# One list schedule for mixers, projections and MLP, with tiles placed late

## The chip, the cores and the metric

The kernel runs on one core of a Trainium2 chip. The metric is the device time of one execution in microseconds. The engines of the core work beside each other, each on its own instruction stream: TensorE (PE, matmuls, with its weight loads shown apart as PEld), VectorE (DVE), ScalarE (ACT), GpSimd (POOL), and SyncE (SP), which here only issues DMAs. Matrix products are accumulated in PSUM, whose banks have to be read out by DVE or ACT before they are used again.

## The reference

One inference step of a layer with four mixers in parallel, over 128 context and 512 latent tokens of width 1024 (640 token rows in all):

```python
h = rmsnorm(x, norm1_g) * (1 + scale1) + shift1
proj = h @ w_in
(a_q, a_i, a_ff, a_fb, a_g, b_q, b_k, b_v, b_g, b_af, b_ab,
 c_x, c_g, d_b, d_c, d_v) = jnp.split(proj, points, axis=-1)
o_a, sf_a = hgrn2_mixer(a_q, a_i, a_ff, a_fb, a_g, ...)      # gated linear recurrence
o_b, sf_b = gla_mixer(b_q, b_k, b_v, b_g, b_af, b_ab, ...)   # gated linear attention
o_c, sf_c = rglru_mixer(c_x, c_g, ...)                       # gated recurrent block
o_d = short_conv_mixer(d_b, d_c, d_v, sconv_w, rows)         # gated short convolution
mix = jnp.concatenate([o_a, o_b, o_c, o_d], axis=-1) @ w_out
x = x + gate1 * mix
h2 = rmsnorm(x, norm2_g) * (1 + scale2) + shift2
ff = jnp.square(jax.nn.relu(h2 @ mlp_w1)) @ mlp_w2
x = x + gate2 * ff
```

Scale, shift and gate come from a conditioning vector for each kind of token. The recurrences of A and B run in both directions in chunks of 32 tokens; their final states are outputs, too. A last rmsnorm follows. w_in is 1024 wide on the input side, w_out 1024x1024, the MLP 1024 to 4096 and back.

## The kernel before, in words

Each large product is made in fp32r with split operands: a matrix is rounded to a high part (`hi`), the rest is the low part (`lo`), and hi·hi, hi·lo and lo·hi are added in PSUM. So a weight tile costs a DMA, a rounding copy (ACT or DVE) and a subtraction (DVE) before PE can use it. The scores and states of the recurrences, the head norms, sums and transposes are plain fp32 matmuls.

The program has four stretches.

1. Start, to about 50 us: x is loaded, normed, transposed and split (`hhi`, `hlo`); first projections. An order written by hand (`START`, under `manual_schedule`, L416) sets it.
2. Mixers and input projections, about 50 to 324 us. The string `PLAN` (L33) lists the units: a projection of 128 columns (`proj_cm`, L229, into the PSUM tiles `pja`, `pjbqk`, `pjcx`, ..., `pjdv`, `pjdb`; values `vi` and `vbv` at L599 to L601), or one step of a generator that runs a mixer (A0, A1, B, RG). Scores are `sA`, `sB` (L699, L726), sums for the conditioning `ap` (L273, L279), gates of the recurrent block `rg` (L869), head norms `hna`, `hnb` (L808). Instructions are written in the order of the list; the framework's own scheduler then orders them on each engine, and places tiles at the point where the program asks for them.
3. Out-projection, 324 to about 367 us. `out_mm` (L1055, its matmuls at L1070) handles one of 5 token tiles and one of 8 row blocks k of w_out; blocks are taken in the order `kord` = 4, 5, 0, 1, 2, 3, 6, 7. Half of the blocks have their split weights in tiles `xh`, `xl` (loaded as `wq` by `wo_x`, L1014 to L1016), half in `vh`, `vl` (loaded as `w2raw` by `wo_v`, L1020). Blocks 4, 5, 2, 3 are in `xh`, blocks 0, 1, 6, 7 in `vh`. `wq` lies in a pool that is opened behind the close of the mixers' and the projections' pools (`ml_`, `hw_`), `w2raw` and `vh` in one that only needs the earlier mixer pool.
4. MLP, to 820 us, with sums and differences of blocks of h2 and of w1 that save products (`product`, matmuls at L1241) and a second product (`mm2`, L1321). Its weights are `wq` to `xh`, `xl` (L1224, L1225) and `w2raw` to `vh`, `vl` (L1311, L1312); operands derived from h are `yh`, `yl`, `ohi`, `t` (L1137, L1138).

Stretches 3 and 4 are ordered by the class `Plan` (L53 to L143): each unit is added with an engine, a duration and what it reads and writes; PE's units stay chained in the order of the program; the rest are placed by a list schedule, earliest start first, and among the startable the one with the earliest latest-start time. Units were bundles (one `out_mm` of 6 matmuls is one entry of 1.36 us).

Of the kernel before, what the change touches and what calls it, by code (L numbers as in the profile page):

```python
# [51 lines left out]

class Plan:  # L53
# [3 lines left out]
    def __init__(self):  # L57
        self.ops = []
        self.writer, self.readers = {}, {}

    def add(self, eng, dur, fn, r=(), w=(), late=0.0):
        i = len(self.ops)
        deps = set()
        for k in r:
            if k in self.writer:
                deps.add(self.writer[k])
        for k in w:
            if k in self.writer:
                deps.add(self.writer[k])
            deps.update(self.readers.get(k, ()))  # L70
        for k in r:
# [5 lines left out]
        self.ops.append((eng, dur, fn, deps, late))  # L77

    def emit(self):
        n = len(self.ops)  # L80
        hop = 0.13
        pe_t, t = {}, 0.0
        for i, (eng, dur, *_) in enumerate(self.ops):
            if eng == "PE":
                pe_t[i] = t
                t += dur
        end = t
        latest = [pe_t.get(i, end + 10.0) for i in range(n)]
        prev = {}
        lastpe = None  # L90
        for i in range(n):
            if i in pe_t:
                prev[i] = lastpe
                lastpe = i
        for i in range(n - 1, -1, -1):
            eng, dur, fn, deps, late = self.ops[i]
            for d in deps:
                e2, d2, _, _, l2 = self.ops[d]
                need = latest[i] - d2 - l2 - (hop if e2 != eng else 0.0)
                latest[d] = min(latest[d], need)  # L100
        left = [len(o[3]) for o in self.ops]
        after = [[] for _ in range(n)]
        for i, o in enumerate(self.ops):
            for d in o[3]:
                after[d].append(i)
            if prev.get(i) is not None and prev[i] not in o[3]:
                left[i] += 1
                after[prev[i]].append(i)
        ready = {}
        at = [0.0] * n  # L110
        free = {}
        for i in range(n):
            if not left[i]:
                ready.setdefault(self.ops[i][0], []).append(i)
        order = []
        while len(order) < n:
            best = None
            for eng, xs in ready.items():
                if not xs:
                    continue  # L120
                f = free.get(eng, 0.0)
                s = max(f, min(at[i] for i in xs))
                i = min((x for x in xs if at[x] <= s + 1e-9), key=lambda x: (latest[x], x))
                if best is None or s < best[0]:
                    best = (s, eng, i)
            s, eng, i = best
            ready[eng].remove(i)
            _, dur, fn, deps, late = self.ops[i]
            free[eng] = s + max(dur - 0.08, 0.05)
            order.append((s, i))  # L130
            for j in after[i]:
                e2 = self.ops[j][0]
                d = s + dur + late + (hop if e2 != eng else 0.0) if i in self.ops[j][3] else free[eng]
                if e2 == eng and eng != "SP" and i in self.ops[j][3]:
                    d = free[eng]
                at[j] = max(at[j], d)
                left[j] -= 1
                if not left[j]:
                    ready.setdefault(e2, []).append(j)
        self.order = order  # L140
        for _, i in order:
            self.ops[i][2]()
# [3 lines left out]
def hybrid_step_kernel(ctx: ExitStack, tc: tile.TileContext, A: dict, O: dict):  # L146
# [42 lines left out]
    def lnexp(after):  # L189
        with tc.issue_after(after.ins):  # L190
            ld = act.preload_act_table_set("natural_log_exp_and_others")
        with tc.issue_after(ld.ins):
            yield
# [253 lines left out]
    me = me_.enter_context(tc.tile_pool(name="mixe", bufs=1, reuse_waits="tile"))  # L447
    mp = ml_.enter_context(tc.tile_pool(name="mixl", bufs=1, side="right", reuse_waits="tile"))
# [7 lines left out]
    def sub(t, g, off, ap):  # L456
        v = t[:, g, off:off + 1]
# [489 lines left out]
    for u in PLAN:  # L947
# [10 lines left out]
        if u == "q1":  # L958
            psS_stack.close()
            psB = stB.enter_context(tc.tile_pool(name="psB", bufs=2, space=PS, reuse_waits="tile"))  # L960
    grow1 = gate_rows("gt1", nc.sync)
    for j in jobs.values():
        assert next(j, None) is None
    me_.close()
    lp = ctx.enter_context(tc.tile_pool(name="mlp", bufs=1, reuse_waits="tile"))
# [16 lines left out]
    ls = ctx.enter_context(tc.tile_pool(name="mlps", bufs=1, reuse_waits="tile"))  # L982
    stB.close()
    psA_.close()
    psN = ctx.enter_context(tc.tile_pool(name="psN", bufs=1, space=PS, reuse_waits="tile"))
# [4 lines left out]
    def tiles(p, n, shape, nm, dt=F32):  # L990
        return [p.tile([128] + shape, dt, name=f"{nm}{i}", tag=f"{nm}{i}") for i in range(n)]
# [14 lines left out]
    XA = {}  # L1006
# [614 lines left out]
```

## Time and profile before

| | |
|---|---|
| median of 3 runs | 828.07 us (824.24 to 829.06) |
| the profiled execution's own time | 829.46 us |
| its span, first to last instruction | 827.7 us |
| mean granted TensorE clock over the span | 0.989 of full speed |
| busy: PE, DVE, ACT, POOL | 783.6, 581.2, 425.9, 23.5 us |
| DMA | 97.78 MB, 118 GB/s on average |

Busy time says how long an engine had an instruction in work. PE's busy time overstates what it needed, since matmuls overlap and their ends are modelled; where PE is back to back, the distance between starts is the better measure. A wait is put down to the instruction that ended last before it was over. The chain of waits follows the program back from its last instruction, at each step to what released it.

### The profile page before, as it was taken

To read this page: it belongs to the slowest core of one execution; us is meant where nothing else is said; L and a number is where in the kernel's file an instruction comes from. 1 tells how busy PE (TensorE), PEld (TensorE's weight loads), DVE (VectorE), ACT (ScalarE), POOL (GpSimd) and SP (SyncE) were. 2 spreads that over 40 slices of the span, in tenths; PEclk is the share of its full clock that TensorE was granted. 3 is DMA by queue.
4 is the path that set the end of the run, shared out by engine and by line. 5 is a ranking of instruction groups with operands and counts; after the bars stand their busy time and mean duration, and the time that the engine had idled before them with its cause. 6 is when DMAs were issued, how large, how long until landed. Compare 5 with 4: busy or idle time off the path is not lost.

```text
span 827.7 us, 13723 instructions
## 1 busy us (share of the span) xinstructions
PE 783.6 (95%) x5536; PEld 688.0 (83%) x5536; DVE 581.2 (70%) x1061; ACT 425.9 (51%) x708; POOL 23.5 (3%) x48
## 2 busy tenths in 40 slices
PE   4999999999989987999799999999999999999996
PEld 3798987777777987888797989989899898988984
DVE  4789989767875466177888898947567475563787
ACT  7543559688396323156566734717247173471533
POOL 0040000101010000000000000000000000000001
PEclk9999999999999999999999999999999999999998
DMA  9723333342411522434444534444132041330313
GB/s 369 286 96 116 104 127 109 112 152 57 151 52 55 123 81 81 174 128 139 166 153 128 178 103 153 115 113 130 51 114 91 16 138 51 101 103 1 126 53 127
DMA packets 33695, 97.78 MB, mean 118 GB/s; under 512 B 8672, under 2 KB 9696, under 8 KB 29024
## 3 DMA queue, kind: packets, MB, share of 16 engines
q1 hardware_dynamic: 32544, 95.72, 34.7%
q10 hardware_dynamic: 576, 1.00, 0.4%
q8 instruction: 43, 0.70, 0.3%
q0 software_dynamic: 512, 0.20, 0.1%
q14 instruction: 20, 0.16, 0.1%
HBM read 91.44 MB, written 5.46 MB: 117 GB/s over the span
## 4 chain that ended last, share of the span: by engine, by line
PE 65%; DVE 14%; ACT 12%; DMA 6%; issue 2%; SPq 0%; DVEq 0%; ACTq 0%
PE ps L1321 26%; PE ps L1241 20%; PE ps L1070 5%; ACT QbB L199 2%; PE pjcx L229 2%; PE pjdb L229 2%; PE pja L403 2%; DMA w2raw<-in_wout_dram 1%; DMA wq<-in_w_dram 1%; DVE QbB L197 1%; PE pjdv L229 1%; DMA rawdb<-in_win_dram 1%; PE ap L273 1%; DVE StA L771 1%; ACT QbA L199 1%
## 5 line engine op out<-in xcount | busy, mean ns | idle before, releaser
L1321 PE MATMUL ps<-vh,olo 128*128 128x512 f32 x640 | 173.7, 390 | 0.5 <-DVE olo L1267 0.5
L1321 PEld LDWEIGHTS ps<-vh,olo 128*128 128x128 f32 x640 | 119.5, 188 | 26.0 <-DVE olo L1267 1.7
L1321 PE MATMUL ps<-vl,olo 128*128 128x512 f32 x320 | 99.2, 389 | 0.0
L1311 ACT ACTIVATE vh<-w2raw 128x1024 fp32r<-128x1024 f32 x32 | 33.7, 1057 | 121.6 <-PE ps L1321 114.1
L1241 PE MATMUL ps<-yh,xh 128*128 128x320 f32 x256 | 79.8, 312 | 1.0 <-DVE rb L1283 1.0
L1241 PE MATMUL ps<-yh,xl 128*128 128x320 f32 x256 | 79.7, 311 | 0.0
L1241 PE MATMUL ps<-yl,xh 128*128 128x320 f32 x256 | 79.6, 311 | 0.0
L1516 DVE TENSOR_TENSOR h<-ps,h 128x512 f32<-128x512 f32 x60 | 38.5, 685 | 56.7 <-PE ps L1321 56.3
L1224 ACT ACTIVATE xh<-wq 128x512 fp32r<-128x512 f32 x96 | 58.4, 625 | 24.0 <-PE ps L1241 17.6
L1225 DVE TENSOR_TENSOR xl<-wq,xh 128x512 fp32r<-128x512 f32 x96 | 64.1, 686 | 9.3 <-ACT xh L1224 8.9
L1321 PEld LDWEIGHTS ps<-vl,olo 128*128 128x128 f32 x320 | 60.1, 188 | 12.6
L1241 PE MATMUL ps<-ohi,xh 128*128 128x320 f32 x256 | 58.6, 316 | 4.6 <-ACT rb L1280 4.6
L1241 PEld LDWEIGHTS ps<-yh,xh 128*128 128x128 f32 x256 | 48.6, 190 | 1.6 <-DVE rb L1283 1.3
L1241 PEld LDWEIGHTS ps<-yl,xh 128*128 128x128 f32 x256 | 48.6, 190 | 0.3
L1241 PEld LDWEIGHTS ps<-yh,xl 128*128 128x128 f32 x256 | 48.5, 189 | 0.0
L1241 PEld LDWEIGHTS ps<-ohi,xh 128*128 128x128 f32 x256 | 43.8, 192 | 5.5 <-ACT rb L1280 5.1
L1280 ACT ACTIVATE rb<-ps 128x320 f32<-128x320 f32 x64 | 27.3, 428 | 40.5 <-PE ps L1241 38.9
L1312 DVE TENSOR_TENSOR vl<-w2raw,vh 128x1024 fp32r<-128x1024 f32 x32 | 38.7, 1221 | 11.2 <-ACT vh L1311 10.5
L1241 PE MATMUL ps<-ohi,xl 128*128 128x320 f32 x128 | 40.2, 314 | 0.0
L1267 DVE TENSOR_TENSOR olo<-rb,olo 128x640 fp32r<-128x640 f32 x32 | 26.3, 821 | 16.1 <-ACT olo L1266 16.1
L1241 PE MATMUL ps<-t,xh 128*128 128x320 f32 x128 | 28.6, 310 | 1.2 <-DVE rb L1283 1.2
L1283 DVE TENSOR_TENSOR rb<-ps,rb 128x320 f32<-128x320 f32 x48 | 23.3, 487 | 7.0 <-PE ps L1241 6.1
(438 smaller groups left out, 1731.7 us busy)
## 6 DMA issues: line engine op xcount, KB each, us to landing
ar<-in_ada_w_dram SPq DMA_DIRECT2D x20, 1024.0 KB, 4.8
wq<-in_w_dram SPq DMA_DIRECT2D x72, 256.0 KB, 3.5
w2raw<-in_w_dram SPq DMA_DIRECT2D x32, 512.0 KB, 4.3
big<-in_ada_g_dram SPq DMA_DIRECT2D x8, 512.0 KB, 3.6
x<-in_x_dram SPq DMA_DIRECT2D x5, 512.0 KB, 5.6
big<-in_x_dram SPq DMA_DIRECT2D x5, 512.0 KB, 4.4
x1d<-big SPq DMA_DIRECT2D x5, 512.0 KB, 2.7
xa<-x1d SPq DMA_DIRECT2D x5, 512.0 KB, 4.5
```

The costliest lines, as they stand in the source:

```text
L199: act.activation(out, src, AF.Copy)
L229: pe.matmul(ps[:, n, :320], wt[:, k, c0:c0 + 128], h[:, k, s], start=(k == 0 and wt is hi and h is hhi), stop=stop)
L1070: pe.matmul(ps[n], lh, w[ix[n]] if nm == "x" else w[ix[0]][:, HALVES[n]], start=(ki == 0 and i == 0), stop=(ki == 7 and i == 2))
L1224: plan.add(ACT, aa_(512), lambda: act.activation(hi, src, AF.Copy), sk, [("xh", s)])
L1225: plan.add(DVE, tt(512), lambda: dve.tensor_tensor(lo, src, hi.bitcast(F32), OP.subtract), sk + [("xh", s)], [("xl", s)])
L1241: pe.matmul(PT[b][n][:, :HT], w[:, k, :], h[:, k, :], start=(start and k == 0 and i == 0), stop=(k == 3 and i == 2), skip_group_check=True)
L1267: plan.add(DVE, tt(640), lambda: dve.tensor_tensor(AL[i], r, AH[i].bitcast(F32), OP.subtract), rk + [("ah", i)], [("al", i)])
L1280: plan.add(ACT, 0.44, lambda: act.activation(dst, src, AF.Copy), [r], [w])
L1311: plan.add(ACT, aa_(1024), lambda hi=hi, raw=raw: act.activation(hi, raw, AF.Copy), rk, [("vh", i)])
L1312: plan.add(DVE, tt(1024), lambda hi=hi, lo=lo, raw=raw: dve.tensor_tensor(lo, raw, hi.bitcast(F32), OP.subtract), rk + [("vh", i)], [("vl" ...
L1321: pe.matmul(PT[b][c.start // 512], lh[i][:, ts_], rh[i][:, c], start=(i == 0 and pi == 0), stop=(i == 3 and pi == 2))
L1516: DVE, tt(512), lambda: dve.tensor_tensor(a, PT[b][n], a, OP.add), [pk[n], ("h", n)], [("h", n)]))
```

## The change

The class `Plan` now records everything behind the start: mixers, input projections, the splitting of their outputs, the loads and splits of w_out, out-projection and MLP. Calls on the engines go through proxies (`Engine`, `Queues`) that record one instruction each with a modelled cost. Tiles of the recorded part are placeholders (`LateTile`) and get a real place when the schedule reaches their first user; the order in which tiles of one tag take slots stays that of the program. Pools are opened by events in the schedule. PE's instructions of the mixers may be put in any order that the data allow; from the out-projection on they stay chained. The loads of ACT's tables are put in by the schedule, at a price of 1.28 us, and a switch counts as 6 us of lateness. In the out-projection, blocks 4, 5, 0, 1 now have `vh`, `vl`, and blocks 2, 3, 6, 7 `xh`, `xl`. In the very last tile, both halves' last multiplication come after both halves' sums.

```diff
+class LateTile:
+    def place(self):
+        if self.got is None:
+            shape, dtype, name, tag, bufs = self.args
+            self.got = self.pool.real.tile(shape, dtype, name=name, tag=tag, bufs=bufs)
+        return self.got
...
+    def cost(self, eng, op, out, ins, a, k):
...
+        if eng == "PE":
+            if op == "transpose":
+                return 4 * self.size(ins[0]) / 2400, 0.0
+            cols = self.size(a[2])
+            if a[2].dtype == F32R:
+                return cols / 2400 + 0.0134, 0.0
+            rows = (out.like if isinstance(out, Late) else out).shape[0]
+            return (4 * cols / 2400 + 0.01) * min(1.0, rows / 128), 0.0
...
+    def add(self, eng, dur, fn, ins=(), outs=(), mb=0.0, sets=None, after=()):
...
+        if eng == "PE":
+            if self.chain and self.last_pe is not None:
+                order.add(self.last_pe)
+            self.last_pe = i
...
     def emit(self):
...
-        hop = 0.13
+        hop = {"PE": 0.22, "ACT": 0.08, "DVE": 0.08, "POOL": 0.15, "SP": 0.0, "X": 0.0}
+        tail = [2.0 + 2.9 * o[5] if o[5] else 0.0 for o in ops]
...
+            if eng == "ACT":
+                i = min(xs, key=lambda x: (latest[x] + (6.0 if ops[x][6] and held not in ops[x][6] else 0.0), x))
+            else:
+                i = min(xs, key=lambda x: (latest[x], x))
...
+            if mb:
+                link = max(link, end) + 2.9 * mb
+                end = link + 2.0
...
-    ml_.close()
-    hw_.close()
-    rp = ctx.enter_context(tc.tile_pool(name="mlpr", bufs=1, side="right", reuse_waits="tile"))
...
+    rp.opened = ls.opened = plan.event(open_rest, [lp.opened] + wpool.users + mp.users + on_rows)
+    psN.psum = True
+    psN.opened = plan.event(open_psum, psA.users + psB.users + on_first)
...
-    wo_x(2, 0)
-    wo_v(0, 0)
-    wo_x(1, 4)
-    wo_v(3, 2)
+    wo_v(2, 0)
+    wo_v(0, 2)
+    wo_x(1, 0)
+    wo_x(3, 4)
...
-    plan = Plan()
...
-        plan.add(PE, 1.36, emit, keys(nm + "h", ix) + keys(nm + "l", ix) + [("oh", k // 2), ("ol", k)],
...
+    plan.chain, plan.last_pe = True, None
```

In the changed program every recorded instruction is issued from one line, L205 (the loads of ACT's tables from L358). Three places of its order:

PE at the end of the projections, before. `pjdb` is the last projection, L1070 the out-projection:

```order
L229 MATMUL pjdb_3423<-hhi,hidb 128x320 x2
L229 MATMUL pjdb_3423<-hlo,hidb 128x320 x2
L229 MATMUL pjdb_3423<-hhi,lodb 128x320 x2
L1070 MATMUL ps_0_3618<-xh_3549,ohi_3485 128x512
L1070 MATMUL ps_1_3619<-xh_3550,ohi_3485 128x512
```

The same place of the change:

```order
L205 MATMUL pjdb_3450<-hlo,hidb 128x320 x2
L205 MATMUL hnb_3534<-o2b_3431,con 128x320
L205 MATMUL pjdb_3450<-hhi,lodb 128x320 x2
L205 MATMUL ps_0_3560<-vh_3279,ohi_3248 128x512
L205 MATMUL ps_1_3562<-vh_3279,ohi_3248 128x512
L205 MATMUL ps_0_3560<-vl_3290,ohi_3248 128x512
```

The first operand of the out-projection is now a `vh`. 48 matmuls on `vh` and `vl` stand ahead of the first one on `xh`. The loads and splits of the four `vh` blocks stand, on SP, ACT and DVE, ahead of the last projection's outputs.

PE in the mixers, before: a projection of mixer A, then a group of 20 scores:

```order
L229 MATMUL pja_741<-hhi,hia_627 128x320 x2
L229 MATMUL pja_741<-hlo,hia_627 128x320 x2
L229 MATMUL pja_741<-hhi,loa_628 128x320 x2
L699 MATMUL sA_801<-QbA_710,KA_794 32x64 x20
L273 MATMUL ap_943<-ar_945,scx 32x256 x8
```

Such a group in the change:

```order
L205 MATMUL pja_681<-hhi,loa_665 128x320
L205 MATMUL pja_683<-hhi,loa_665 128x320
L205 MATMUL sA_831<-QbA_626,KA_725 32x64 x5
L205 MATMUL pja_681<-hhi,loa_665 128x320
L205 MATMUL pja_683<-hhi,loa_665 128x320
L205 MATMUL sA_831<-QbA_626,KA_725 32x64 x2
```

Groups of scores are now cut up and laid between the matmuls of the projection. From the first `pja` to the last `pjdb`, both programs have the same 1104 fp32r and 760 fp32 matmuls; unbroken stretches of fp32 ones number 61 before and 96 in the change, 35 of which are a single matmul. From one matmul to the next the output tile changes 198 times before and 659 times in the change.

ACT in the early MLP, before. `rb` reads a product out of PSUM, `vh` is a weight's rounding copy, `ohi` from `h` an operand of a product:

```order
L1311 ACTIVATE vh_3495<-w2raw_3505 128x1024
L1224 ACTIVATE xh_3551<-wq_3567 128x512
L1137 ACTIVATE ohi_3484<-rb_3571 128x4x128
L1224 ACTIVATE xh_3549<-wq_3565 128x512
L1137 ACTIVATE ohi_3483<-h_3574 128x4x128
L1280 ACTIVATE rb_3571<-ps_0_3614 128x320
```

The same place of the change:

```order
L205 ACTIVATE rb_4024<-ps_0_3732 128x320
L205 ACTIVATE ohi_3537<-rb_4189 128x4x128
L205 ACTIVATE vh_3279<-w2raw_3250 128x1024
L205 ACTIVATE ohi_3252<-h_3792 128x4x128
L205 ACTIVATE xh_3620<-wq_3597 128x512
L205 ACTIVATE rb_4189<-ps_0_3572 128x320
```

An `rb` and the `ohi` from `rb` now stand ahead of the `vh`; the `ohi` from `h` and another `rb` still stand behind it.

## Rows read from the trace of the kernel before

**Rows 1.** The page: busy us, share of the span and instructions of each engine.

```profile
PE 783.6 (95%) x5536; PEld 688.0 (83%) x5536; DVE 581.2 (70%) x1061; ACT 425.9 (51%) x708; POOL 23.5 (3%) x48
```

**Rows 2.** Stretches: length, busy us of each engine (instructions), granted clock, DMA share, GB/s.

```profile
50.00:105.00 55.00, 53.95 (x686) 51.21 (x685) 53.67 (x114) 21.59 (x31) 5.69 (x10) 1.00 0.29 100
50.00:324.00 274.00, 262.39 (x2639) 225.90 (x2638) 208.93 (x401) 156.20 (x250) 16.64 (x32) 1.00 0.30 97
324.00:336.00 12.00, 7.39 (x21) 5.41 (x20) 6.26 (x11) 4.18 (x7) 0.00 (x0) 0.72 0.80 272
...
404.00:418.00 14.00, 9.41 (x44) 8.87 (x44) 9.38 (x17) 5.80 (x12) 0.00 (x0) 0.76 0.30 101
418.00:820.00 402.00, 398.69 (x2181) 358.60 (x2179) 280.93 (x472) 192.60 (x313) 2.40 (x1) 1.00 0.32 100
```

**Rows 3.** PE's waits: total us, times, longest.

```profile
PE ps L1070 <- ACT xh L1015: 4.6, 1, 4.6
PE ps L1241 <- ACT rb L1280: 4.6, 1, 4.6
PE sB L699 <- ACT QbB L199: 3.0, 7, 0.7
```

**Rows 4.** Timeline at the out-projection's entry: start, us, engine, instruction, [idle before <-releaser].

```profile
323.94 0.46 PE L229 MATMUL pjdb<-hhi,lodb 128*128 128x320 f32 x2
...
324.91 0.48 DVE L587 TENSOR_TENSOR od<-dy,pjdb 128x320 f32<-128x320 f32 x1
...
328.33 2.56 ACT L1015 ACTIVATE xh<-wq 128x512 fp32r<-128x512 f32 x4 [13.55 <-DMA wq<-in_wout_dram]
328.99 2.63 DVE L1016 TENSOR_TENSOR xl<-wq,xh 128x512 fp32r<-128x512 f32 x4 [2.22 <-ACT xh L1015]
...
329.01 1.41 PE L1070 MATMUL ps<-xh,ohi 128*128 128x512 f32 x2 [4.61 <-ACT xh L1015]
```

**Rows 5.** The chain of waits, pieces there: start, us, what.

```profile
324.43 3.82 DMA wq<-in_wout_dram
329.01 32.18 PE ps L1070 x126
```

**Rows 6.** Timeline of the early MLP, around PE's stall.

```profile
401.18 0.38 SPq L1044 DMA_DIRECT2D w2raw<-in_w_dram  x1
...
407.13 1.06 ACT L1311 ACTIVATE vh<-w2raw 128x1024 fp32r<-128x1024 f32 x1 [3.23 <-DMA w2raw<-in_w_dram]
...
409.65 0.61 ACT L1137 ACTIVATE ohi<-h 128x512 fp32r<-128x512 f32 x1
...
410.17 0.41 ACT L1280 ACTIVATE rb<-ps 128x320 f32<-128x320 f32 x1
...
410.64 0.63 PE L1241 MATMUL ps<-ohi,xh 128*128 128x320 f32 x1 [4.59 <-ACT rb L1280]
```

**Rows 7.** PE's timeline in the mixers, at changes between fp32r and fp32.

```profile
110.11 0.46 PE L229 MATMUL pjcx<-hhi,locx 128*128 128x320 f32 x2
110.49 1.32 PE L699 MATMUL sA<-QbA,KA 128*32 128x64 f32 x80
111.75 0.56 PE L229 MATMUL pjbqk<-hhi,hibqk 128*128 128x320 f32 x2
112.15 0.46 PE L229 MATMUL pjbqk<-hlo,hibqk 128*128 128x320 f32 x2
112.44 0.45 PE L229 MATMUL pjbqk<-hhi,lobqk 128*128 128x320 f32 x2
...
116.19 0.46 PE L229 MATMUL pjbqk<-hhi,lobqk 128*128 128x320 f32 x2
116.49 1.04 PE L747 MATMUL ktA<-con,GA 128*128 128x128 f32 x8
117.28 0.53 PE L229 MATMUL pjbqk<-hhi,hibqk 128*128 128x320 f32 x2
117.65 0.46 PE L229 MATMUL pjbqk<-hlo,hibqk 128*128 128x320 f32 x2
```

More of the change, by code (lines that the diff above doesn't have):

```diff
@@ new lines, with __init__, tile @@
+class LatePool:
+    def __init__(self, plan, real=None, opened=None, psum=False, bufs=1):
+        self.plan, self.real, self.opened, self.psum, self.bufs = plan, real, opened, psum, bufs
+        self.slots, self.users = {}, []
+    def tile(self, shape, dtype, name=None, tag=None, bufs=None):
+        t = LateTile(self, shape, dtype, name, tag or name, bufs or self.bufs)
+        ap, step = [], 1
+        for n in reversed(shape[1:]):
+            ap.insert(0, [step, n])
+            step *= n
+        return Late(t, bass.AP(tensor=self.plan.like, offset=0, ap=[[step, shape[0]]] + ap), dtype)
@@ L95, in emit @@
         for i in range(n - 1, -1, -1):
-            eng, dur, fn, deps, late = self.ops[i]
+            eng, dur, _, deps, order, mb, _ = ops[i]
             for d in deps:
[L98 to L101, printed above, removed]
+                e2, d2 = ops[d][0], ops[d][1]
+                latest[d] = min(latest[d], latest[i] - d2 - tail[d] - (hop[e2] if e2 != eng else 0.0))
@@ L102, in emit @@
+            for d in order:
+                latest[d] = min(latest[d], latest[i] - (ops[d][1] if ops[d][0] == eng else 0.0))
+            for d in back.get(i, ()):
+                latest[d] = min(latest[d], latest[i] - ops[d][1] - tail[d] - hop[ops[d][0]])
+        left = [len(o[3]) + len(o[4]) for o in ops]
         after = [[] for _ in range(n)]
-        for i, o in enumerate(self.ops):
+        for i, o in enumerate(ops):
             for d in o[3]:
[L105 to L108, printed above, removed]
@@ L112, in emit @@
         for i in range(n):
             if not left[i]:
-                ready.setdefault(self.ops[i][0], []).append(i)
-        order = []
-        while len(order) < n:
+                offer(i)
+        link, held, out = 0.0, None, []
+        while len(out) < n:
             best = None
+            assert any(ready.values()), [(i, ops[i][0], [k.args[2:4] for k in starts[i]]) for i in waiting]
             for eng, xs in ready.items():
@@ L138, in emit @@
                 if not left[j]:
[L139 to L142, printed above, removed]
+                    offer(j)
+            if again:
+                for j in sorted(waiting):
+                    offer(j)
+        self.order = out
+        for _, i, load in out:
+            if load:
+                self.nc.scalar.preload_act_table_set(load)
+            ops[i][2]()
 @with_exitstack
@@ L1073, in out_mm @@
-        plan.add(PE, 1.36, emit, keys(nm + "h", ix) + keys(nm + "l", ix) + [("oh", k // 2), ("ol", k)],
-                 [("ps", b, 0), ("ps", b, 1)])
+        ps = PT[bank_of[t]]
+        ts_ = slice(128 * t, 128 * t + 128)
+        lhi, llo = oT["hi"][k // 2][:, k % 2, ts_], oT["lo"][k][:, ts_]
+        for i, (lh, part) in enumerate(((lhi, 0), (lhi, 1), (llo, 0))):
+            for n in range(2):
+                pe.matmul(ps[n], lh, wo[k][n][part], start=(ki == 0 and i == 0), stop=(ki == 7 and i == 2))
@@ L1492, in hybrid_step_kernel @@
             unit(2 * g + i, 2 * i)
-        if g == NG - 1:
+        if last:
             start_last()
-        pair = [bank_pair() for _ in range(2)]
+        pair = [PT[bank_pair()] for _ in range(2)]
         for i0 in (0, 3):
```

746 lines of the change are left out of this document (398 added, 348 removed).

## The prediction

> **What bounds the kernel now.** I read the page's busy times first, then PE's waits, then the stretches in which PE idles, and last the timelines there. PE is busy 783.6 of 827.7 us and the next engine, DVE, 581.2 [rows 1]: the time can fall only where PE waits, runs at a lower clock, or has its work laid out at a higher price. In the long MLP stretch little is left: 398.69 of 402 us busy, 3.3 us idle or 0.8% [rows 2]. In the mixers it is 262.39 of 274, so 11.6 us idle or 4.2%, with DVE busy 208.9 and ACT 156.2; for the first 55 us DVE is busy 53.67 [rows 2]. These idle pieces are short: the largest group by releaser is seven waits of scores `sB` for `QbB`, 3.0 us together, none over 0.7 [rows 3]. Two waits are long, 4.6 us each [rows 3]: one at the entry of the out-projection, one early in the MLP. In the two stretches around them the granted clock is 0.72 over 12 us and 0.76 over 14 us, elsewhere in the mixers and the MLP 1.00 [rows 2]. The engine was idle before both falls, and what it lost there is 12 × 0.28 and 14 × 0.24, 3.4 us each.
>
> **The entry of the out-projection.** The last two projection matmuls start at 323.94 [rows 4]; at 0.147 us each (0.29 for a pair, 112.15 to 112.44 in [rows 7]) PE is free at 324.23. It starts again at 329.01 [rows 4], 4.8 us later. What it waits for is a DMA of `wq`, issued at 324.43, once the projections' pool was free, with 3.82 us to land [rows 5], and then ACT's `xh`. The clock then costs at most 3.4 us, some 0.3 of it while PE still waited, and the first pair of matmuls waits for the second `xh`, 0.3 us. That is 8.2 us.
>
> The change lets PE begin with 48 matmuls on `vh` and `vl`, whose loads and splits were ahead of the last projection before, too, so no work is added by the exchange. A 512-column matmul takes (32.18 − 3.4)/126 = 0.228 us [rows 5], so these last 10.9 us. In that cover the `wq` load lands (4.3 us after the last projection matmul, if issued as now), ACT makes four `xh` in 2.56 and DVE the last `xl` 0.65 later [rows 4]: 7.5 us. The four `xh` and `xl` of the next block are 3 us further, and are wanted at 16 us. If the cover is gone (a late `vh`), the 4.8 us are back. Late next is PSUM: the second token tile's accumulators stand where `od` reads the last projection. `od` ended 1.2 us after PE was free [rows 4], and the first token tile covers 1.4. In the new order `od` stands behind a longer piece of the convolution on DVE; I bound that from 0 to 2 us and take 1. Gain 7.2, bounds 5.0 to 8.2.
>
> **The stall in the early MLP.** ACT waits 3.23 us for `w2raw`, issued at 401.18, to make a `vh`; behind that, in order, stand `ohi` (409.65) and `rb` (410.17), and PE starts at 410.64 [rows 6]. In the change an `rb` and an `ohi` have moved ahead of this `vh`, but another `ohi` and `rb` still stand behind it. I take 1.2 us (two of ACT's pieces of 0.6 us) and the clock falls as before. Bounds: 0, and the whole 4.6 + 3.4 = 8.0.
>
> **The mixers: price of the switches.** A pair of projection matmuls takes 0.29 us start to start. Before the scores it takes 0.38 (110.11 to 110.49), after them 0.40 (111.75 to 112.15); before the transposes 0.30, after them 0.37 [rows 7]. So a stretch of fp32 matmuls inside fp32r ones costs 0.09 to 0.20 us over its own work. The order has 96 such stretches for 61: 35 × 0.09 to 0.20 is 3.2 to 7.0 us, I take 5. The Trainium skill, page TensorE: Matmul & The Clock Gate, section on the step-by-step phases (Part 2), lets the drain of one matmul overlap the fill of the next and names no exception for a change of type; by it these 5 us would be nothing and the sum 5 us lower. The rows above show a price at each of the four places but one, so I keep it.
>
> **The mixers: the idle time.** The 11.6 us can go to the 0.8% that the same class reaches in the MLP (2.3 us, so −9.3), or grow. I take half away, −5.8: the MLP's feeding work is independent of PE's, while a mixer's chain runs PE, ACT, DVE and back. The cuts of groups into pieces of 2 to 8 give each piece its own start. Their wait was part of the 11.6 already.
>
> **The rest.** Fewer loads of ACT's tables lie beside PE's work (ACT 156 of 274). At the end one multiplication of the size of an `xl`, 0.65 us [rows 4], moves behind the last sum, partly beside ACT's square: +0.3, bounds 0 and 0.65; if nothing covers it, 0.65.
>
> **Sum.** 829.46 (the profiled execution) − 7.2 − 1.2 + 5 − 5.8 + 0.3 = 820.6. That execution lies 1.4 above the median 828.07, so 819.2, and I say 819. What a measurement of this kernel can tell from no change is about 1%, 8.3 us: faster means under 819.8, slower above 836.4.
>
> **The rivals.**
>
> *The mixers come out as well as the MLP.* Switches at 3.2, idle −9.3, the entry −8.2, the rest as above: 829.46 − 8.2 − 1.2 + 3.2 − 9.3 + 0.3 = 814.3, less 1.4, 813; with the MLP's stall wholly gone as well, 806. For it: DVE has room after the first 55 us, and the class leaves 0.8% in the MLP [rows 2]. Against it: in those 55 us DVE is full. The Trainium skill, page Perfetto Trace Analysis, Optimization Strategy, says that where the most-contended engine changes over time, interleaving the regimes can help; by that rule this case is the likelier one. 21%.
>
> *Slower: fp32 stretches that wait for their operands.* PE takes its matmuls in order. A stretch of scores put in where a modelled time says that `QbB` or `QbA` is there makes PE wait if ACT or DVE is late, and whatever projection matmuls are behind it wait, too. Now it is 11.6/61 = 0.19 us a stretch. At 0.30 with 96 stretches it is 28.8 us, 17.2 more instead of 5.8 less: 842. It decides from 0.24 a stretch (23.1 us, 836.4). For it: all of [rows 3]'s short waits are of this kind, and DVE has no slack at the start, so an error in its modelled costs is not made good. Against it: the order chooses by data that are due, and the waits were short under the order before as well. 22%. With 0.19 a stretch kept, it would be 18.2 us and 831.6: 6%.
>
> *The entry wait stays in another form.* The pool's waits (the accumulators behind the convolution, or the first `vh` late) hold PE as long as `wq` did: 819 + 7.2 = 826. For it: `od` sits behind a longer DVE chain. Against: its bound of 2 us, and long lead of the `vh` loads. 9%.
>
> *The clock falls inside the mixers.* Each fall of the two seen cost 3.4 us [rows 2]; five of them make 819 + 17 = 836. For it: the change writes to another accumulator 659 times from one matmul to the next, 198 before, which makes more places to wait. Against: the clock held 1.00 through 274 us with 11.6 us of idle pieces [rows 2]. Only 2%. The Trainium skill, page TensorE: Matmul & The Clock Gate, section on psum-queue depth-cycling, says that changing accumulators each step can leave PE idle in small pieces and make the clock swing; by that rule this chance would be larger, and no stretch of this trace shows it.
>
> **How the numbers follow.** The forecast has 40%, with 813 to 825 of its own (the bounds of entry, switches and tail). About half of it, 21%, lies under 819.8. Faster: 21 + 21 = 42%. Same: 19 + 9 + 6 + 2 = 36%. Slower: 22%. The range reaches from 805 (the first rival with the stall gone) to 839 (the slower rival's nearer half); out of it stand about a half of that rival and a few per cent below.
>
> **What would show it.** At the out-projection's start PE goes from the last `pjdb` to `ps<-vh` with under 2 us between, and the granted clock there stays 1.00; a wait over 4 us says that the entry failed. In the early MLP the fall to 0.76 stays, and `vh` still ends PE's wait; if not, the stall was shorter than I took it. PE's idle in the mixers against 11.6 us, and the time from the first mixer matmul to the last projection matmul against 274 us, tell the forecast (about 273) from the first rival (268) and the slower one (296). Starts of pairs around cut groups should show 0.09 to 0.20 over 0.29. Wrong would be above all a mixer stretch whose DVE or ACT work comes later than the order meant.

## The result, and the profile after

The changed kernel takes **873.15 us** (median of 4 runs, 872.05 to 876.5) against 826.15 for the kernel before (median of 4): ratio 1.057, 95% interval 1.052 to 1.062. The prediction was 819, with 805 to 839 as its range, so neither the time nor the sign was right.

The profiled execution, the longest of the four, has a span of 874.7 us against 827.7, 47.0 more. Cut at the starts of the same matmuls in both traces (the last `pjq`, the last `pjdb`, the first and the last product of the MLP) and at the end, the difference lies here (us):

| stretch of PE | before | after | change |
|---|---|---|---|
| start, to the last `pjq` | 57.80 | 58.22 | +0.42 |
| mixers, to the last `pjdb` | 266.29 | 306.73 | +40.44 |
| out-projection, to the first product | 66.84 | 63.37 | −3.47 |
| MLP, first to last product | 400.71 | 410.84 | +10.13 |
| last accumulations and end | 36.04 | 35.55 | −0.49 |

The page's busy times and the chain of waits of the changed kernel; the first line answers to [rows 1]:

```profile
PE 803.9 (92%) x5536; PEld 697.1 (80%) x5536; DVE 580.9 (66%) x1061; ACT 420.0 (48%) x704; POOL 24.3 (3%) x48
...
PE 65%; DVE 14%; DMA 11%; ACT 7%; issue 2%; SPq 0%; DVEq 0%; ACTq 0%
```

PE is busy 20 us longer with the same matmuls (lower clock, more switches), and idle for the rest. DMA is now 11% of the chain; it was 6% before. PE's waits (in all, times, longest), which answer to [rows 3]:

```profile
PE pjdb L205 <- DVE hidb L205: 12.0, 1, 12.0
...
PE ps L205 <- DVE rb L205: 8.2, 2, 8.0
PE ps L205 <- ACT rb L205: 5.6, 3, 3.4
PE pja L205 <- DVE hia L205: 5.1, 1, 5.1
PE ps L205 <- DVE od L205: 2.5, 1, 2.5
```

Three waits are new: 12.0 us in the last mixer, 8.0 in the middle of the MLP, 5.1 at the start of the mixers. (The helper that records all operations is one line, L205, so the tiles tell them apart.) Each is followed by a lower granted clock, as the windows of the stretches show (length, busy us and instructions of PE, PEld, DVE, ACT, POOL, granted clock, DMA share, GB/s); the first line is the whole of the mixers and answers to the 274 us in [rows 2]:

```profile
50.00:366.00 316.00, 283.49 (x2642) 235.73 (x2641) 209.02 (x403) 152.85 (x249) 11.73 (x22) 0.96 0.30 88
...
62.00:69.00 7.00, 5.37 (x19) 5.06 (x20) 6.72 (x15) 4.35 (x7) 0.00 (x0) 0.52 0.14 21
...
328.00:345.00 17.00, 6.52 (x23) 6.12 (x24) 10.15 (x13) 3.59 (x4) 0.00 (x0) 0.51 0.42 97
...
566.00:576.00 10.00, 4.94 (x25) 4.94 (x26) 6.44 (x11) 2.43 (x5) 0.00 (x0) 0.66 0.37 106
```

**The wait of 12.0 us.** `pjdb`'s weights (`rawdb`) are split on DVE before PE can use them. The queue of SP, DVE and PE there:

```profile
309.66 0.40 SPq L205 DMA_DIRECT2D rowgt<-gt  x1
310.15 1.15 SPq L205 DMA_DIRECT2D w2raw<-in_wout_dram  x2
311.35 0.91 SPq L205 DMA_DIRECT2D big<-in_x_dram  x2
312.30 0.47 SPq L205 DMA_DIRECT2D rowgt<-gt  x1
317.31 5.34 SPq L205 DMA_DIRECT2D rawdb<-in_win_dram  x1
...
336.31 1.23 DVE L205 CAST hidb<-rawdb 128x2048 fp32r<-128x2048 f32 x1 [6.63 <-DMA rawdb<-in_win_dram]
...
337.59 0.90 PE L205 MATMUL pjdb<-hhi,hidb 128*128 128x320 f32 x2 [12.00 <-DVE hidb L205]
```

`rawdb`, 1 MB, lands 19.0 us after its issue (6.8 in the kernel before). Ahead of it on the queue stand 2 MB of other loads (two `w2raw`, two `big`) and two stores of the first gate's rows, each 4 KB written in 1024 pieces of 4 B. The same order is in the MLP for the second gate:

```profile
556.69 0.74 SPq L205 DMA_DIRECT2D rowgt<-gt  x1
557.64 1.42 SPq L205 DMA_DIRECT2D wq<-in_w_dram  x1
559.11 0.59 SPq L205 DMA_DIRECT2D rowgt<-gt  x1
...
569.18 0.69 DVE L205 TENSOR_TENSOR s<-wq,wq 128x512 f32<-128x512 f32 x1 [9.00 <-DMA wq<-in_w_dram]
...
571.06 0.64 PE L205 MATMUL ps<-yh,xh 128*128 128x320 f32 x1 [8.01 <-DVE rb L205]
```

A quarter of a megabyte of `wq` takes 11.5 us there. The kernel before makes the same stores. After those of the second gate its DMA moved 19 GB/s over 12 us while PE missed nothing:

```profile
534.00:546.00 12.00, 12.00 (x54) 9.94 (x54) 7.45 (x14) 1.62 (x3) 0.00 (x0) 1.00 0.38 19
```

So the cost was hidden there, and I had not put a price on it. That is the first suspect.

**The wait of 5.1 us.** DVE after the change, then before, at the start of the mixers:

```profile
58.13 0.89 DVE L205 COPY qA<-pjq 128x384 f32<-128x384 f32 x2 [9.76 <-PE pjq L619]
...
63.06 0.42 DVE L205 CAST hia<-rawa 128x512 fp32r<-128x512 f32 x1
```

```profile
49.90 1.84 DVE L197 CAST hia<-rawa 128x512 fp32r<-128x512 f32 x2 [0.51 <-PE pja L403]
```

The plan's clock begins at zero with all engines free and `pjq` finished. On the chip PE still has 18 us to go then. So copies of `pjq` came out first on DVE's and ACT's queues, and DVE stands 9.76 us behind one of them with `hia`, ready to be made, in the same queue. That is the second suspect. The third is the switches between fp32 and fp32r, which the prediction had.

### The profile page after: what moved, and what is told of

Same layout as the page of the kernel before. It is cut to its first block, busy times and chain, and to the rows that moved or that the text cites. A ratio compares the mean times of both kernels' runs of the same rounds, so it can differ in the third digit from the quotient of the medians.

```text
span 874.7 us, 13743 instructions
## 1 busy us (share of the span) xinstructions
PE 803.9 (92%) x5536; PEld 697.1 (80%) x5536; DVE 580.9 (66%) x1061; ACT 420.0 (48%) x704; POOL 24.3 (3%) x48
## 4 chain that ended last, share of the span: by engine, by line
PE 65%; DVE 14%; DMA 11%; ACT 7%; issue 2%; SPq 0%; DVEq 0%; ACTq 0%
PE ps L205 39%; DMA w2raw<-in_w_dram 3%; DMA wq<-in_w_dram 2%; DMA rawdb<-in_win_dram 2%; DVE big L205 2%; DVE xl L205 2%; PE pjcx L205 2%; PE pjbqk L205 2%; PE pjdc L205 2%; PE sA L205 2%; ACT QbB L205 2%; PE pjq L619 2%; PE pja L619 2%; PE pjdb L205 1%; PE vbv L205 1%
## 5 line engine op out<-in xcount | busy, mean ns | idle before, releaser
L205 PE MATMUL ps<-vh,olo 128*128 128x512 f32 x680 | 186.7, 391 | 0.1
L205 PEld LDWEIGHTS ps<-vh,olo 128*128 128x128 f32 x680 | 127.5, 188 | 27.2 <-ACT h L205 0.8
L205 ACT ACTIVATE vh<-w2raw 128x1024 fp32r<-128x1024 f32 x36 | 38.1, 1058 | 144.3 <-PE ps L205 115.5
L205 PE MATMUL ps<-vl,olo 128*128 128x512 f32 x320 | 99.3, 390 | 0.0
L205 ACT ACTIVATE xh<-wq 128x512 fp32r<-128x512 f32 x104 | 63.9, 626 | 62.1 <-PE ps L205 47.7
L205 PE MATMUL ps<-yh,xh 128*128 128x320 f32 x256 | 80.8, 316 | 10.7 <-DVE rb L205 8.2
L205 PE MATMUL ps<-yl,xh 128*128 128x320 f32 x256 | 80.0, 313 | 0.0
L205 PE MATMUL ps<-yh,xl 128*128 128x320 f32 x256 | 79.9, 312 | 0.0
L205 DVE TENSOR_TENSOR xl<-wq,xh 128x512 fp32r<-128x512 f32 x104 | 69.7, 688 | 10.6 <-ACT xh L205 10.1
L205 DVE TENSOR_TENSOR h<-ps,h 128x512 f32<-128x512 f32 x60 | 38.6, 686 | 57.2 <-PE ps L205 56.8
L205 PEld LDWEIGHTS ps<-vl,olo 128*128 128x128 f32 x320 | 60.1, 188 | 12.6
L205 PE MATMUL ps<-ohi,xh 128*128 128x320 f32 x256 | 58.4, 315 | 4.7 <-ACT rb L205 4.7
L205 PEld LDWEIGHTS ps<-yh,xh 128*128 128x128 f32 x256 | 49.1, 192 | 12.0 <-DVE rb L205 8.7
L205 DVE TENSOR_TENSOR vl<-w2raw,vh 128x1024 fp32r<-128x1024 f32 x36 | 43.8, 1222 | 15.6 <-ACT vh L205 14.9
L205 ACT ACTIVATE rb<-rb 128x640 f32<-128x640 f32 x64 | 47.3, 739 | 8.1 <-DVE rb L205 6.4
L205 PEld LDWEIGHTS ps<-yl,xh 128*128 128x128 f32 x256 | 49.1, 192 | 0.3
L205 PEld LDWEIGHTS ps<-yh,xl 128*128 128x128 f32 x256 | 49.0, 191 | 0.0
L205 PEld LDWEIGHTS ps<-ohi,xh 128*128 128x128 f32 x256 | 43.8, 192 | 5.5 <-ACT rb L205 5.5
L205 PE MATMUL ps<-ohi,xl 128*128 128x320 f32 x128 | 40.3, 315 | 0.0
L205 DVE TENSOR_TENSOR olo<-rb,olo 128x640 fp32r<-128x640 f32 x32 | 26.3, 822 | 19.7 <-ACT olo L205 19.7
L205 ACT ACTIVATE rb<-ps 128x320 f32<-128x320 f32 x64 | 26.9, 420 | 6.2 <-PE ps L205 6.2
L205 DVE TENSOR_TENSOR rb<-ps,rb 128x320 f32<-128x320 f32 x48 | 23.4, 487 | 8.2 <-PE ps L205 8.2
```

Of the source, the lines that this page charges most:

```text
L205: return fn(*[r(x) for x in a], **{w: r(v) for w, v in k.items()})
```

## The experiments

Each ratio is to the kernel before, run on the same chip beside the experiment. The experiments ran on five chips (1 to 4, 5 to 8, 9 to 12, 13 and 14, and 15 together), on which the medians of the kernel before are 827.81 to 829.25 us. So a difference of medians between two of these groups, or to the change, is known to some 4 us, the half-width of a ratio's interval; inside a group it is known better.

**1. The pieces of the row stores.** The changed kernel, each store writing 128 pieces of 64 B, in an order of elements that is not the reference's; the order of all engines is as in the change.

```
-  q.dma_start(d[cnd:cnd+1, :].rearrange("c (k p) -> p (c k)", p=128), mod[name][:, :, cnd])
+  q.dma_start(d.rearrange("c (p k) -> (c p) k", p=64), mod[name].rearrange("p k c -> p (k c)"))
```

> The change with one edit: each of the four stores that write a gate row to DRAM writes 128 pieces of 64 B instead of 1024 pieces of 4 B (values then lie in another layout, so the gates are wrong; every engine's order stays that of the change). Theory A (the scattered stores slow the transfers behind them): rawdb lands in 7 us instead of 19, PE's 12 us wait before pjdb and the 8 us wait near 563 us fall under 2 us each, with most of the clock loss beside them: 873 to about 848. Rival (those transfers are late because SP reaches them late or the slots come free late): under 5 us gained, 868 or more.

855.13 us, ratio 1.034 (1.030 to 1.038): 18 less. What the DMA did with both loads in the change, and in this run (KB each, median us from issue to landing):

```profile
rawdb<-in_win_dram SPq DMA_DIRECT2D x1, 1024.0 KB, 19.0
rowgt<-gt SPq DMA_DIRECT2D x2, 4.0 KB, 16.6
```

```profile
rawdb<-in_win_dram SPq DMA_DIRECT2D x1, 1024.0 KB, 5.3
rowgt<-gt SPq DMA_DIRECT2D x2, 8.0 KB, 5.3
```

Twice the bytes in an eighth of the pieces land three times as fast, and `rawdb` with them. PE's wait of 12.0 is gone, that of 8.0 is 2.0. The Trainium skill (DMA: Bandwidth & Descriptors, Why small descriptors are slow) gives each descriptor a fixed cost; the direction agrees. That section says nothing of the loads behind them, which is where the time went.

**2. The start.** The changed kernel, the plan's engines free at 9.0, 9.8 and 18.2 us and `pjq` read from 18.2.

```
+  if any(isinstance(k, str) and k.startswith("pjq") for k in r):
+      self.floor[i] = 18.2
...
-  at, free, ready, end_of = [0.0] * n, {}, {}, [0.0] * n
+  at, free, ... = [self.floor.get(i, 0.0) ...], {"PE": 18.2, "ACT": 9.0, "DVE": 9.8, "POOL": 9.0}, ...
```

> The change with one edit: the schedule is told when its engines are free of the start and when pjq is there (SP 0, ACT 9.0, DVE 9.8, PE and pjq 18.2 us) instead of all at time 0. Theory B (the copies of pjq stand first on DVE and ACT and hold both for 8 us): PE's 5.1 us wait at 58 us and the clock fall behind it go, 873 to about 864. Rival (DVE catches up anyway, the list is only shuffled): within 5 us of 873, either way.

871.54 (1.053, 1.050 to 1.057): the wait of 5.1 is gone and `pjcx`, `pjag`, `pjdc` end 6.8 to 6.9 us sooner. The wait for `rawdb` then grew from 12.0 to 13.9, and the last product of the MLP comes 5.1 us sooner. The medians, of two chips, differ by 1.6 only, which by itself would speak for the rival. So the cause is real by the traces, a later wait takes up a part of it, and its worth is not told by this run's time.

**3. The out-projection's entry alone.** The kernel before with the exchange of the w_out slots and nothing else (blocks on `vh`, `vl` first).

```
-  wslots = {4: ("x", (0, 1)), 5: ("x", (2, 3)), 2: ..., 0: ("v", (0,)), 1: ("v", (1,)), ...
+  wslots = {4: ("v", (0,)), 5: ("v", (1,)), 0: ("v", (2,)), 1: ("v", (3,)), 2: ("x", (0, 1)), ...
```

> The kernel before with only the exchange of w_out's slots (blocks 4, 5, 0, 1 in vh, 2, 3, 6, 7 in xh). By the term of the prediction: the entry's 4.8 us wait and the clock fall go, 1 us of PSUM wait stays: 826 to about 819. Rival (the banks or the vh loads are the next wait): 823 to 828.

827.26, ratio 0.998 (0.996 to 1.000). The entry itself did what the prediction's first term says. Before, [rows 4] had a wait of 4.6 and the clock fell. Here, and then in the early MLP:

```profile
325.00:344.00 19.00, 19.00 (x84) 15.53 (x83) 7.61 (x13) 5.00 (x8) 0.00 (x0) 1.00 0.80 277
398.00:415.00 17.00, 14.13 (x51) 13.02 (x52) 12.47 (x22) 8.47 (x18) 0.00 (x0) 0.52 0.36 120
```

The first product starts at 383.6 instead of 390.9, 7.3 us sooner; the 97th is only 2.9 sooner. ACT, DVE and PE tell why:

```profile
393.42 1.28 ACT L1335 ACT_TABLE_LOAD   x1 [2.69 <-DMA gate<-in_ccr_dram]
...
395.90 0.69 DVE L1138 TENSOR_TENSOR ohi<-h,ohi 128x512 fp32r<-128x512 f32 x1 [2.71 <-ACT ohi L1137]
...
398.62 0.60 PE L1241 MATMUL ps<-yh,xh 128*128 128x320 f32 x1 [3.42 <-DVE h L1130]
```

ACT stands for a 1 MB load for the second gate, whose result is first used in the last MLP group, then loads a table for it. An `ohi` is queued behind that, DVE stands 2.71 us for this `ohi`, and the `h` that PE waits for is queued behind it on DVE.

**4. PE in the written order.** The changed kernel with PE bound to the order in which its matmuls are written (`plan.chain` true from the start).

> The change with PE chained in the order of the program from the start on, so PE's instructions of mixers and projections aren't interleaved any more; the rest is scheduled as in the change. Theory C (interleaving fp32 and fp32r, and two projections at once, costs PE its time): 873 to 860 or lower. Rival (the loss is in the transfers and the start, and free order is worth something): 870 to 885.

948.6 (1.146, 1.140 to 1.150), with waits for `ar` of 19.4 us in four. PE's free order is worth 75 us within the change. That the plan orders PE's matmuls freely is not what costs.

**5. The switches.** The changed kernel, the plan preferring the kind of matmul at hand unless the other is due 2 us sooner.

```
...
+  elif eng == "PE":
+      i = min(xs, key=lambda x: (latest[x] + (2.0 if self.kind[x] != self.was else 0.0), x))
+      self.was = self.kind[i]
```

> The change with one rule more: the order prefers the kind of matmul (fp32 or fp32r) that PE has just done, unless the other kind is due 2 us earlier. Stretches of fp32 in the mixers: 58 instead of 96 (before: 61). Theory of the switches (7.3 us of PE's time in the mixers, without waits and clock, over before): about 7 us come back, pjag's last matmul at about 226 instead of 233.4, and the run at 866 if the wait of pjdb for its late load does not take it back, 868 to 871 if it does in part. Rival, that a switch as such costs nothing and the longer steps are operands that come late: same as the change, 873.

870.28 (1.049, 1.045 to 1.053). The last `pjag` starts at 226.3, 7.1 us sooner, as the theory had it. Of that, 4.1 are left at the last `pjdc`, behind a wait of 2.5 us for ACT's `gelu`, and 1.8 at the last `pjdb`, behind the late `rawdb` (a wait of 12.3). At the last product it is 3.4, near the medians' 2.9.

**6 to 8. The three together, one after the other.** The rows go through PE: it transposes the 128x16 tile, ACT copies it, eight stores write two rows of 512 B each, now in the reference's order; the second gate's one MLP group later.

```
-  for cnd in range(2):
-      q.dma_start(d[cnd:cnd+1, :].rearrange("c (k p) -> p (c k)", p=128), mod[name][:, :, cnd])
...
+  pe.transpose(pt[0:16, 0:128], flat(mod[name]), ident)
+  act.activation(r, pt[0:16, 0:128], AF.Copy)
+  for k in range(KT):
+      q.dma_start(d[:, 128 * k:128 * k + 128], r[2 * k:2 * k + 2, :])
```

> The change with the gate rows stored by another way, right in value: PE transposes the 128x16 tile, ACT copies it, and eight stores write rows of 512 B instead of two that write 1024 pieces of 4 B each; the second set is made one group of the MLP later. Theory of the scattered stores: as with the contiguous stores before, 855 (852 to 858); rawdb lands 5 to 8 us after its issue instead of 19.0, no wait of pjdb over 2 us and no wait of 8 us in the MLP. Rival, that the run with contiguous stores gained by something else than the pieces' size: 873.

> The change with the row stores by transposes and with a plan that knows when the engines are free at the start. If the start's gain was given back to the late rawdb alone, it counts now: 855 - 7 = 848, with PE's first wait after pjq gone and pjdb's last matmul near 341. Rival, that it is given back wherever the loads and the slots come at their own pace: 855.

> The change with all three: stores by transposes, a plan that knows the start, and the preference for the kind of matmul at hand (53 stretches of fp32). If the three causes add up: 873 - 18 - 7 - 7 = 841, and what is left over the kernel before, about 13, is short waits in the mixers. If the switches are no cause of their own: 848.

863.43 (1.040, 1.035 to 1.044), 853.69 (1.029, 1.025 to 1.033) and 842.43 (1.016, 1.011 to 1.021). The first misses its 855 by 8. The start brings 9.7 and the switches 11.3 more, each above the 7 expected: with `rawdb` on time, the mixers kept them. Of what the first run had too much, 6 us stand at the entry of all three (69.5 to 70.0 us from the last `pjdb` to the first product, 63.4 in the change); in the last of them:

```profile
324.67 2.38 SPq L207 DMA_DIRECT2D rowgt<-grgt  x8
327.15 0.83 SPq L207 DMA_DIRECT2D w2raw<-in_wout_dram  x2
...
336.26 1.22 PE L207 MATMUL ps<-vh,ohi 128*128 128x512 f32 x2 [5.02 <-ACT vh L207]
340.04 1.22 PE L207 MATMUL ps<-vl,ohi 128*128 128x512 f32 x2 [2.56 <-DVE vl L207]
```

My small tile for the rows was in the mixers' pool, so the store had to go out before the next pool opened, and `w2raw` stood behind it.

**9. That tile in another pool.**

```
-  r = me.tile([16, 128], F32, name=f"gr{name}") ...
+  r = tmp(f"gr{name}")[0:16, 0:128] ...
```

> The run with stores, start and switches (842.4), with one thing mended: the small tile of the transposed gate row stood in the mixers' own pool, so the store had to be issued before the out-projection's pool could open, and w2raw stood behind it on SP (issued at 327.15, PE waits 5.0 for vh and 2.6 for vl, clock lower until 344). Now it stands in another pool and the four w2raw are ordered ahead of the store. Theory: waits for vh and vl under 2 us together, first product 6 us sooner, 836. Rival, that the out-projection's entry is bound by the operands of the last mixer (ohi, olo at 333 to 338), so the load is hidden: 842.

833.37 (1.006, 1.004 to 1.008), 9 less. SP now, and the clock over the entry:

```profile
289.24 0.86 SPq L207 DMA_DIRECT2D w2raw<-in_wout_dram  x2
...
299.85 1.71 SPq L207 DMA_DIRECT2D w2raw<-in_wout_dram  x2
326.94 2.36 SPq L207 DMA_DIRECT2D rowgt<-grgt  x8
```

```profile
318.00:345.00 27.00, 26.16 (x136) 22.00 (x135) 15.20 (x27) 6.90 (x12) 0.22 (x4) 1.00 0.34 108
```

Three causes are now away, and with them some 40 us of what the change lost. The rival, that the last mixer's operands bind the entry, falls.

**10 to 12. The second gate's loads later.** In the plan they wait for the first MLP group: in the kernel before with the slots of experiment 3, in experiment 9's kernel, and in the kernel before alone. The edit of the kernel before is shown; in experiment 9's kernel each of these loads is ordered behind PE's last recorded instruction.

```
-  dma(flat(GATE), bass.AP(...src...), 1.0, [], [("gate",)])
+  dma(flat(GATE), bass.AP(...src...), 1.0, [("al", 3)], [("gate",)])
-  dma(wt, A["ada_g"][i], 0.5, [], [("big", 0)])
+  dma(wt, A["ada_g"][i], 0.5, [("al", 3)], [("big", 0)])
```

> The kernel before with the exchanged slots of w_out (the run that gained 7.3 us at the out-projection's entry and gave most of it back in the early MLP), and with the loads for the second gate (1 MB gate<-in_ccr, issued at 384.90 there, and the ada_g loads) ordered behind the first MLP group. Theory: the gain was given back because ACT stood 2.7 us for that 1 MB and then loaded a table (1.28), and the wq loads behind it landed late; without it the wait of 3.6 us at 394.89 and the one of 0.8 at 402 go and the clock stays up: 820 to 822, ratio 0.99. Rival, that the norm of the last tokens is bound by its own chain on DVE and ACT: 827.

> The run with the row tile elsewhere, and the loads for the second gate behind the first MLP group. Theory: the early stall of the MLP (3.6 us and some 3 us of clock) goes: 6 us under the run without it, 830. Rival, own chain of the norm: no difference to it.

> The kernel before with the loads for the second gate behind the first MLP group and nothing else. Theory: ACT's wait of 3.23 us for w2raw (issued at 401.18, behind the gate's load and ACT's work on it) goes, with PE's wait of 4.6 and the clock's fall: 820 to 823. Rival, that w2raw is late for its own reasons (its slot comes free late): 828.

831.95 (1.004, 1.003 to 1.006), 828.51 (0.999, 0.998 to 1.001) and 837.42 (1.010, 1.008 to 1.012). The second is as quick as the kernel before. The other two missed, upwards. The early stall did shrink: the 97th product starts at 403.0 in the first, after 410.6 before and 407.8 with the slots alone. But the gate's work, and its row stores, moved to another place:

```profile
645.39 2.11 SPq L1044 DMA_DIRECT2D rowgt<-gt  x2
...
651.71 0.53 SPq L1044 DMA_DIRECT2D w2raw<-in_w_dram  x1
```

```profile
645.00:650.00 5.00, 5.00 (x24) 4.14 (x23) 3.24 (x10) 0.63 (x1) 0.00 (x0) 1.00 0.24 5
650.00:655.00 5.00, 5.00 (x28) 4.41 (x27) 3.74 (x4) 1.49 (x2) 0.00 (x0) 1.00 0.24 14
655.00:660.00 5.00, 5.00 (x36) 5.00 (x35) 1.78 (x3) 0.96 (x2) 0.00 (x0) 1.00 0.47 48
660.00:665.00 5.00, 0.46 (x4) 0.20 (x2) 0.06 (x1) 1.15 (x2) 0.00 (x0) 0.93 1.02 389
```

For 15 us after the stores the DMA moves 5 to 48 GB/s; `w2raw` is behind them and PE waits 8.6 us (8.4 in the kernel before alone, at 667). It is the first suspect again, this time in the order of the kernel before.

**13 and 14. The rows by transposes in these kernels.** Experiment 10's kernel, and the kernel before alone, with the second gate's rows stored as in experiment 6.

> The kernel before with the exchanged w_out slots, the second gate's loads behind the first MLP group, and the second gate's rows stored as 16 rows of 512 B after a transpose, one group later. In the run without the last step (831.95) PE waited 8.6 us at 660.15, after the row stores issued at 645.39 had left the DMA at 5 to 48 GB/s until 660 and w2raw, issued at 651.71, landed late. Theory: that wait and the lower clock behind it (some 3 us) go, 820, ratio 0.99. Rival, that w2raw is late there because eight loads of the gate now lie in the same place: 832.

> The kernel before with nothing but the second gate's rows stored as rows of 512 B after a transpose. Theory: the scattered stores cost only where a load behind them is waited for, and PE has no wait over 0.7 us between 436 and 730 in the kernel before: no change, 827 to 830. Rival, that they cost by themselves wherever they stand: 815 to 820.

825.26 (0.996, 0.994 to 0.997): the wait of 8.6 is gone. And 834.46 (1.008, 1.006 to 1.010): neither theory. The trace shows a part of why it is slower: a group later the eight stores and the gate's 1 MB come just where the next group's weights are fetched.

```profile
714.78 4.09 SPq L1044 DMA_DIRECT2D rowgt<-big  x8
719.91 0.35 SPq L1044 DMA_DIRECT2D gate<-rowgt  x1
720.31 0.42 SPq L1044 DMA_DIRECT2D wq<-in_w_dram  x1
```

PE's wait from 732 on is 2.3 us for 1.0 before, and the clock is 0.83 over the ten us in which it falls, together some 3 of the 6 us; the rest is not traced. Since the stores also moved by a group, this run does not tell what the scattered ones cost where they stood.

**15. The stores where SP has nothing to issue.** Experiment 13's kernel with the transpose ahead of that group's accumulations.

> As the run with exchanged slots, later gate loads and transposed rows (825.3), with the transpose and the stores put ahead of that group's accumulations: they leave SP about 680, where it has nothing to issue until 704, not at 706 to 714 ahead of the next group's wq. Theory: the wait of 2.3 us at 723 and the lower clock behind it (0.83 over 10 us, 1.7 us) fall back to the kernel before's 1.2 us without a fall: 822. Rival, that the wait is wq's own: 825.

**819.94**, ratio 0.990 (0.988 to 0.993), the fastest of all. The stores leave at 688.72, the gate's load at 691.99, and SP's next load is due at 703.04; PE's wait at 723 is 0.8 us. In this kernel the entry's gain is kept: the first product comes 7.1 us sooner than in the kernel before, the last one 9.6. No run has the gate's moves without the exchange, so what each is worth in this kernel is not separated.

## Why the prediction was wrong, point by point

**The step that failed** is the mixers' idle time: "I take half away, −5.8", bounded by −9.3 or "grow", with no price on growing. PE's idle time there went from 11.6 us (274 − 262.39, [rows 2]) to 32.5 (316.00 − 283.49): 20.9 more, not 5.8 less. I argued from the class of short waits, `sB` for `QbB` in [rows 3], and asked whether each would be a little shorter or longer. What came were two long waits of another kind: one queue that stands behind a copy the plan takes for ready (5.1), one load behind slow stores (12.0). The 15.4 us that are left over 96 stretches are 0.16 each, so the slower rival, at 842 with 22% and short waits of 0.30 a stretch as its mechanism, was not it either. Nor was half of the idle time there to be taken: in experiment 9, without the two long waits, PE still idles 12.7 of 280 us.

```profile
50.00:330.00 280.00, 267.32 (x2640) 228.74 (x2639) 207.80 (x402) 150.80 (x247) 10.83 (x22) 0.99 0.28 98
```

The rival with 2%, a clock that falls inside the mixers, came true as a consequence: 0.96 over the mixers for 1.00 before. The falls at 62 and 328 us followed the two long waits. It did not come from the cutting as such: in experiment 7, with 95 stretches but no wait over 1.8 us in the mixers, the clock stayed 1.00 from 50 to 342 us.

**What was left out** is the row stores. They were in the list of what the change moves, and their place on SP against `rawdb` and `wq` can be read from the order beforehand; their effect on loads behind them could be read from the kernel before (19 GB/s over 12 us). I looked for waits of PE, and where nothing waited I did not look. Experiments 1, 10 and 13 show the mechanism in both orders: −18 us in the change, 8.6 us of wait made and taken away in the kernel before. This is also the MLP's +10.1, for which the sum had no term: in experiment 1 the MLP takes 402.9 us, 2.2 over before.

**The switches**, +5 with bounds 3.2 to 7.0, had the right sign and were too small, and what costs is narrower than I took it. Four records of fp32 matmuls of full width (`hnb`, 128*128) between fp32r ones, in the kernel before:

```profile
311.43 0.45 PE L229 MATMUL pjdv<-hhi,lodv 128*128 128x320 f32 x2
311.72 1.24 PE L808 MATMUL hnb<-o2b,con 128*128 128x320 f32 x4
...
313.09 0.46 PE L229 MATMUL pjdv<-hlo,hidv 128*128 128x320 f32 x2
```

From 311.43 to 313.09 it is 1.66 us. Two pairs of the projection take 0.59 of it; the 1.07 that are left are 0.27 for each of the four, and 0.27 is also their median distance inside such a stretch. So the change of type costs nothing here. The eight of the transposes in [rows 7], 116.19 to 117.65, come out at 0.87 in the same way, 0.11 each, which is their distance inside a stretch, too. The 0.09 that I read there, from the steps next to them alone, is no price. The scores are different; their outputs have 32 rows (128*32). In the change:

```profile
107.16 0.46 PE L205 MATMUL pjcx<-hlo,hicx 128*128 128x320 f32 x2
107.54 0.77 PE L205 MATMUL sA<-QbA,KA 128*32 128x64 f32 x40
...
108.63 0.45 PE L205 MATMUL pjcx<-hhi,hicx 128*128 128x320 f32 x2
```

These 40 take 1.47 − 0.59 = 0.88 us, and the 80 in [rows 7], 110.11 to 112.15, take 2.04 − 0.59 = 1.45. Forty more cost 0.57, so 0.31 of a stretch does not depend on their number. Stretches with outputs of 32 or 64 rows number 41 before and 69 in the change; at 0.31 each, 28 more are an estimated 9 us. From experiment 7 to 8 they fall from 68 to 38, and the mixers get 12.0 us shorter, 3.6 of it idle time; the rest is 0.28 for each. The rule that the prediction took from the Trainium skill (TensorE: Matmul & The Clock Gate, the step-by-step phases), by which a switch would cost nothing, is borne out for outputs of full width and not for the narrow ones. Another page of the Trainium skill, TensorEngine Tiling (Array Packing), Key Properties, says that a change of tiling mode drains the engine; the trace agrees, with the 0.31 us at the scores. Whether the type adds to that is open, since no narrow matmul of this kernel is fp32r.

**The entry**, −7.2 with bounds 5.0 to 8.2: as a mechanism right. Alone it gave 7.3 us at the first product (experiment 3). In the change PE waited 2.5 us for DVE's `od`, which I had bounded by 2, and the clock fell to 0.86 over 12 us, for which the sum had no term, so 3.5 were left. (The `wq` load of that sum lands 4.1 us after the last projection matmul by [rows 4], not 4.3, which changes nothing.) And what the sum did not ask is what PE meets 60 us later: by [rows 6] ACT and DVE were late there already, so an earlier PE waits longer.

**The early MLP's stall**, −1.2: the wait itself was 3.4 us for 4.6 before, as forecast, and the clock 0.79 over 16 us for 0.76 over 14. But a new wait of 1.6 us for `h` came ahead of it, and from the first product to the 97th it took 20.4 us for 19.7 before, so nothing was gained. I did not see that the second gate's load was part of it; with that load later, 4.9 us came from experiment 9 to experiment 11.

**The end**, +0.3: from the last matmul to the end 8.4 us, 8.6 before. The sign was wrong, at a size that decides nothing.

By differences of medians along experiments 6 to 9, the change's loss is: 18.8 the row stores (873.15 − 863.43 and the 9.1 that my misplaced tile cost), 9.7 the start, 11.3 the switches, together 39.8. By the ratios, each to the kernel before on its own chip, the same steps are 23, 9 and 10, so the first share is known to some 4 us only, and all of them hold for this order of taking the causes away. The 4.5 us that are left (833.37 to 828.87) are not traced to one cause; cut as in the table, experiment 9's trace has +5.6 in the mixers, −6.5 in the out-projection and +3.0 in the MLP against the kernel before.

## What to carry to other kernels

A list schedule is as good as what its model starts from and what it knows of the queues: give it the time at which each engine is really free, and look at each DMA that is moved together with the loads that now stand behind it. A slow store, a load far ahead of its use or a table load cost nothing here while nothing waited behind it, so price it where it will stand, not where it stood. And a gain ahead of a stretch that ACT or DVE sets is only kept if that stretch is loosened as well: the same exchange was worth 1 us alone, and the kernel in which the gate's loads and stores were moved as well is 8 us quicker.

## What the runs showed of the hardware

- 8 KB in two stores of 4-byte pieces held the DMA queue for 10 to 15 us: 5 to 48 GB/s, at a DMA share of 0.24 to 0.47, with up to a megabyte of loads behind them. That all 16 engines are slow, not only those that carry a store, is what the landing of `rawdb` suggests (19.0 us); the share of each was not measured.
- A stretch of fp32 matmuls whose outputs have 32 rows, between fp32r matmuls of full width, cost 0.31 us over its own work. A stretch of fp32 matmuls of full width cost nothing over its own work (1.07 us for four, 0.27 each).
- A lower clock followed each of PE's long waits (5.1, 8.0 and 12.0 us) and stood at 0.51 to 0.66 of full speed in the 7 to 17 us shown, the rest of the wait in them included; it had been at the upper of its two levels, 2.4 GHz, before, and 0.51 is nearly all at the lower, 1.2 GHz.
